# Two row scalings moved to VectorE, a token table and negated scores in a two-block kernel

## The chip, the cores and the metric

The kernel runs on one core of a Trainium2 chip. The metric is the device time of one execution in microseconds (us); the number given for a kernel is the median of its runs, and every run is one launch of the whole program.

## What is computed

The reference takes a sequence of 1024 tokens of width 1024 through two blocks. The part of the first block that matters here ends with a router and 32 experts:

```python
x = x + g1[:, None, :] * mix
h = modulate(x, sh2, sc2)          # rms_norm(x) * (1 + sc2) + sh2
x = x + g2[:, None, :] * hier_moe(h, ...)

g_prob = softmax(hf @ w_group + b_group)          # 4 groups, the best one is taken
e_logits = hf @ w_router + b_router               # 8 experts in a group, the best two are taken
...
out = segment_sum(ys * row_w[:, None], row_tok)   # two experts' rows come back to each token
```

The second block begins with sliding-window attention with a sink, 16 query heads on 4 key heads, blocks of 128 tokens:

```python
s = q @ k.T * HEAD_DIM ** -0.5 - slope * dist     # outside the window: -inf
m = maximum(max(s), sink)
p = exp(s - m)
denom = sum(p) + exp(sink - m)
o = (p / denom) @ v
```

After it come three further mixers and a feed-forward network, which the change does not touch.

## The kernel before

The program is one instruction stream per engine, planned ahead. A scheduler decides the order of most of it; some stretches are written inside a "manual schedule" context, where VectorE, ScalarE and GpSimd (the profile calls them DVE, ACT and POOL) run exactly in the order of the code. The tokens lie in 8 tiles of 128 rows. SyncE (SP) issues nearly all transfers, in the order of its own list, and indirect DMAs (gathers and scatters by a table of row numbers) are issued on POOL.

**Routing.** `phase2` finishes the output projection: `tile_half` (L807) makes half a tile with 24 matmuls (L812), scales it on DVE (L814) and adds it to `x1[t]` (L815). For each tile the router's logits follow: squares and their sums on ACT (`sq`, L966), the norm (`stat`, L971 and `rstd`, L225/L226), 8 transposes on PE (`tr`, L979) with two copies on ACT (L981), 8 matmuls of 36 columns (`mm`, L986) and one DVE operation (`lg`, L990). `h2_rows` (L1006) makes the modulated rows that the experts will gather, and SP writes them to DRAM (`h2d`, L1015) beside the tile itself (`x2d`, L1016). For tiles 0 to 5 that is two DVE operations on 128x1024 (L1010, L1014). For tiles 6 and 7 it is called with POOL as its engine, at the end of the manual stretch: ACT scales by the norm (L1012), POOL multiplies (L1013) and adds (L1014). The buffer is slot 26 or 27, by the parity of the tile.

`route` (L1021) is a generator of about 18 short DVE operations on two or four tiles' logits (L1037 to L1057), each of which needs the one before. The manual stretch hands them out with `some(n)` between the logits of tiles 6 and 7; then the last two tiles are routed, and `dispatch` (L1069) follows, one long dependent chain. It counts tokens per expert, writes the small integer list `ints` (L1134 to L1136) that SP reads to know which expert's weights to load, and builds the table of tokens: 16 one-hot squares of 128x128 (`soh`), the first six on POOL one by one (L1156), the others on DVE (L1152), and 16 matmuls (L1166) that sum `soh[q]` times `bv[q]` in one bank. The values in `bv` come from `val` (L912), twice the token number less 2048; three DVE operations (L1168, L1171, L1172) add 2048, turn the sum into integers and halve it, and that is `toki`. The first gathers on POOL (L1345) need `toki`, and so does SP: from a certain load on, the order of SP's list is tied to it (`self.hold`, L1172, used at L1316).

**Experts.** `phase4` streams the weights of the experts from DRAM (L1315), splits each into a high and a low part (ACT L1334, DVE L1335), multiplies, and adds the results to `x2d` with scatters on POOL (L1339). The scheduler orders this stage.

**Attention.** The loop at L1797 makes 32 steps (8 query blocks by 4 key heads) in manual order. Step `it` transposes the shares of step `it-3` (`turn`: PE L1773, ACT copy L1775, DVE masked copy L1778), makes the scores of step `it` (`scores`), the shares of step `it-1` (`share`), and the values of step `it-3` (PE L1789, ACT L1837, DVE L1838). `scores` is where the lines of the change lie: 4 custom DVE operations (L1744) add the bias to the scores and keep the row maximum in `am`; L1747 negates the four maxima into `anm`, and L1749 makes `aes`, the sink less the maximum:

```python
V.tensor_tensor_reduce(out=s_[:, i, 0:nk], in0=ps, in1=bias[kv][:, i, k0:256], scale=1.0,
                       scalar=sink[:, h:h + 1], op0=ALU.add, op1=ALU.max, accum_out=m[:, i:i + 1])
nm = self.W("anm", [P, 4])
V.tensor_scalar(nm, m, -1.0, None, op0=ALU.mult)
es = self.W("aes", [P, 4])
V.tensor_sub(es, sink[:, 4 * kv:4 * kv + 4], m)
```

`share` takes four exponentials on ACT with `anm` as their bias (L1757) and one of `aes` (L1759), sums and inverts on DVE (L1760, L1761), and lets POOL add the two halves of the window (L1763) and multiply by the inverse (L1764).

## Time and profile before

| | us |
|---|---|
| median of 3 runs | 2257.21 (2256.58 to 2259.82) |
| the profiled execution | 2255.42 |
| its span, first to last instruction | 2253.6 |
| mean granted TensorE clock in it | 0.962 of full speed |

| engine | busy us | share of the span | instructions |
|---|---|---|---|
| PE (matmul) | 2037.8 | 90% | 10594 |
| DVE | 1506.8 | 67% | 2292 |
| ACT | 905.8 | 40% | 1591 |
| POOL | 914.5 | 41% | 662 |

By time, the execution is: up to 427 us the first mixer, 427 to 538 the output projection, 538 to 590 routing and dispatch, 590 to 1190 the experts, 1190 to 1315 the projection for attention, 1315 to 1438 attention, and from there to 2253 the remaining mixers and the feed-forward network. The busy share is a mean over these stages, each with a limit of its own, so the stages are read one by one. In the chain of work that ended last, PE has 48%, DMA 18%, DVE 16% and "issue" (time in which an engine waited for nothing that the profile shows) 10%.

### The profile page before, as it was taken

Reading aid. Unit: us, or ns where it says so; the run is one execution under the profiler, and the core shown is the slowest. Engines: PE = TensorE matmul, PEld = TensorE weight load, DVE = VectorE, ACT = ScalarE, POOL = GpSimd, SP = SyncE. Lnnn points to the kernel's source line nnn. Section 1 sums busy time; section 2 is a strip of 40 time slices with the busy share of each in tenths; the row PEclk is TensorE's granted clock in tenths of the full one; section 3 lists DMA queues with packets and bytes.
Section 4 is the critical chain, followed back from the end, with each engine's and each line's share of the span. In section 5 each row is a group of like instructions: output and inputs, shape, how many; then the busy total and the mean of one; then the engine's idle time right before and its main releaser. Section 6 shows DMA issues by size and latency. Waiting matters only on the chain.

```text
span 2253.6 us, 30335 instructions
## 1 busy us (share of the span) xinstructions
PE 2037.8 (90%) x10594; PEld 1502.7 (67%) x10594; DVE 1506.8 (67%) x2292; ACT 905.8 (40%) x1591; POOL 914.5 (41%) x662
## 2 busy tenths in 40 slices
PE   4988999997899998998868997899999999989996
PEld 2677888886555654666526884587888787767774
DVE  7688886627454534667525449737787777599998
ACT  2544447412244333545315138634322232244433
POOL 2365252333211131212212027404666666567786
PEclk9999999998799999999989999999999999999998
DMA  7462111315899789999994310321454454575541
GB/s 264 126 187 79 30 37 47 114 55 219 311 389 347 280 302 392 381 342 376 381 341 132 131 29 10 122 94 57 131 185 165 145 186 142 166 269 176 193 153 75
DMA packets 204739, 426.09 MB, mean 189 GB/s; under 512 B 18580, under 2 KB 99202, under 8 KB 204578
## 3 DMA queue, kind: packets, MB, share of 16 engines
q1 hardware_dynamic: 195218, 402.62, 49.6%
q0 software_dynamic: 9360, 21.46, 4.1%
q8 instruction: 85, 1.39, 0.3%
q14 instruction: 76, 0.62, 0.1%
HBM read 361.36 MB, written 65.01 MB: 189 GB/s over the span
## 4 chain that ended last, share of the span: by engine, by line
PE 48%; DMA 18%; DVE 16%; issue 10%; POOL 5%; ACT 3%; SPq 0%; POOLq 0%; DVEq 0%; ACTq 0%
PE a L282 7%; DMA s<-w 6%; PE a L270 4%; PE a L812 4%; DMA x2d<-s,dstp 3%; DMA s<-w_ada 3%; PE t L1949 3%; PE a L1949 2%; PE a L1394 2%; PE r L1949 2%; DVE s L2152 2%; DVE s L1744 2%; PE a L1403 2%; PE t L1403 2%; DVE s L1934 1%
## 5 line engine op out<-in xcount | busy, mean ns | idle before, releaser
L1335 DVE TENSOR_TENSOR s<-s,s 128x1024 fp32r<-128x1024 f32 x168 | 207.2, 1243 | 123.8 <-ACT s L1334 120.4
L282 PE MATMUL a<-s,s 128*128 128x512 f32 x1008 | 243.4, 399 | 10.4 <-ACT s L503 10.4
L1334 ACT ACTIVATE s<-s 128x1024 fp32r<-128x1024 f32 x168 | 176.5, 1058 | 159.3 <-PE t L1394 60.5
L282 PEld LDWEIGHTS a<-s,s 128*128 128x128 f32 x1008 | 189.5, 190 | 52.6 <-ACT s L503 10.8
L1934 DVE TENSOR_TENSOR s<-s,s 128x512 fp32r<-128x512 f32 x154 | 162.5, 1072 | 73.3 <-ACT s L1933 73.3
L1949 PE MATMUL t<-s,s 128*128 128x512 f32 x648 | 162.4, 406 | 14.9 <-DVE s L1934 9.9
L1949 PE MATMUL a<-s,s 128*128 128x512 f32 x708 | 172.2, 393 | 0.3 <-DVE s L1934 0.2
L1345 POOL DMA_INDIRECT s<-h2d,toki x38 | 42.5, 1118 | 295.0 <-PE r L1376 142.4
L1949 PEld LDWEIGHTS t<-s,s 128*128 128x128 f32 x648 | 125.7, 195 | 46.8 <-DVE s L1934 11.4
L1933 ACT ACTIVATE s<-s 128x512 fp32r<-128x512 f32 x154 | 91.4, 623 | 159.4 <-DVE s L1934 71.7
L1949 PEld LDWEIGHTS a<-s,s 128*128 128x128 f32 x708 | 132.7, 188 | 31.4 <-DVE s L1934 0.6
L2152 DVE TENSOR_TENSOR s<-s,s 128x512 fp32r<-128x512 f32 x129 | 139.2, 1115 | 0.0
L1394 PE MATMUL t<-s,s 128*128 128x512 f32 x384 | 119.7, 402 | 3.7 <-DVE s L1478 1.8
L1949 PE MATMUL r<-s,s 128*128 128x512 f32 x492 | 120.2, 394 | 0.1
L1394 PE MATMUL a<-s,s 128*128 128x512 f32 x336 | 108.5, 416 | 8.2 <-DVE s L1478 5.0
L270 PE MATMUL a<-s,s 128*128 128x512 f32 x432 | 107.0, 399 | 2.6 <-DVE s L1593 2.6
L1949 PEld LDWEIGHTS r<-s,s 128*128 128x128 f32 x492 | 92.7, 189 | 21.9 <-DVE s L1934 0.5
L2151 ACT ACTIVATE s<-s 128x512 fp32r<-128x512 f32 x154 | 84.8, 622 | 41.5 <-POOL s L2152 18.2
L2317 PE MATMUL a<-s,s 128*128 128x512 f32 x348 | 94.9, 397 | 3.1 <-DVE s L2338 1.7
L2317 PE MATMUL t<-s,s 128*128 128x512 f32 x348 | 90.8, 399 | 7.5 <-DVE hraw L2329 2.0
L1403 PE MATMUL a<-s,s 128*32 128x256 f32 (+1 forms) x736 | 92.1, 468 | 4.9 <-ACT s L1377 3.0
L812 PE MATMUL a<-s,s 128*128 128x512 f32 x384 | 92.7, 397 | 0.6 <-DVE s L666 0.6
(579 smaller groups left out, 4407.7 us busy)
## 6 DMA issues: line engine op xcount, KB each, us to landing
s<-w SPq DMA_DIRECT2D x384, 512.0 KB
s<-w_ada SPq DMA_DIRECT2D x48, 512.0 KB
s<-ffn_w_gate_up SPq DMA_DIRECT2D x44, 512.0 KB
s<-fd SPq DMA_DIRECT2D x77, 256.0 KB
fd<-s SPq DMA_DIRECT2D x33, 512.0 KB
h2d<-s SPq DMA_DIRECT2D x24, 512.0 KB
s<-w_in SPq DMA_DIRECT2D x22, 512.0 KB
s<-ffn_w_down SPq DMA_DIRECT2D x22, 512.0 KB
```

The costliest lines, as they stand in the source:

```text
L270: nc.tensor.matmul(ps[:m], a[:, k, :], b(k, h), start=(k == 0 and n == 0), stop=(k == KC - 1 and n == 2))
L282: nc.tensor.matmul(ps[h][:m], a[:, k, :], b(k, h), start=(k == 0 and n == 0), stop=(k == KC - 1 and n == 2))
L812: nc.tensor.matmul(ps, a.of(k, t), W[k][:, b], start=(k == 0 and n == 0), stop=(k == 7 and n == 2))
L1334: nc.scalar.activation(hi, raw, AF.Copy)
L1335: V.tensor_sub(lo, raw, hi)
L1394: nc.tensor.matmul(pp[h], a[:, k // 4, s], w[:, h * 512:(h + 1) * 512], start=(k == 0 and n == 0), stop=(k == 7 and n == 2))
L1403: nc.tensor.matmul(p_[M * g:M * g + M, 0:N], x[:, k_, :], w[:, :, g, :], start=(k_ == 0), stop=(k_ == 7))
L1933: A.activation(t[:, 0], src, AF.Copy)
L1934: V.tensor_sub(t[:, 1], src, t[:, 0])
L1949: nc.tensor.matmul(ps, t[:, a, k], xs[k][:, b], start=(k == 0 and n == 0), stop=(k == 3 and n == 2))
L2152: (G if loads[1] % SHARE == SHARE - 1 else V).tensor_sub(u[:, 1], t, u[:, 0])
L2317: nc.tensor.matmul(ps[p], a[:, e, q * P:(q + 1) * P], b[:, f], start=(i == g[0] and n == 0), stop=(i == g[-1] and n == 2))
```

## The change

- The rows of tiles 6 and 7 for the experts are made on DVE alone. Tile 6 goes through `h2_rows` at the head of the manual stretch; tile 7 is multiplied by the modulation in two halves (`scaled`) and finished by one scalar_tensor_tensor once its norm is known. ACT's two scalings and POOL's four operations go. Fewer router steps stand between the logits of tiles 6 and 7, and `stat(7)` comes ahead of `lg(6)`.
- The token table holds tokens less 1024, not twice that, and one DVE operation turns the matmuls' sum into `toki` in place of three.
- POOL makes 3 of the 16 one-hot squares in place of 6, DVE the other 13; the matmuls take them in another order.
- Attention takes negated scores: the keys' factors, the bias, the mask and the sink change sign, the custom operation keeps the minimum, which is `anm` at once, so L1747 goes; `aes` is `anm` less the negated sink; the exponentials take a scale of -1.

```diff
@@ phase2 @@
+            def scaled(h):
+                sl = slice(512 * h, 512 * h + 512)
+                V.tensor_mul(h2[:, sl], self.x1[7][:, sl], self.sc2b[:, sl])
+
             sq(6, 0)
             sq(6, 1)
             stat(6)
             sq(7, 0)
+            self.h2_rows(6, V)
             tile_half(7, 1, W1, self.g1[1])
             steps = self.route(4, 6)
...
+            h2 = self.S(27)
+            scaled(0)
             some(2)
             tr(6, 0)
             tr(6, 1)
             mm(6, "t0")
             tr(7, 0)
-            some(4)
+            some(2)
             sq(7, 1)
             tr(7, 1)
-            some(3)
+            scaled(1)
+            some(2)
+            stat(7)
             lg(6)
-            stat(7)
+            some(2)
             mm(7, "a0")
+            V.scalar_tensor_tensor(h2, h2, self.rr[:, 7:8], self.sh2b, op0=ALU.mult, op1=ALU.add)
+            self.h2_out(7, h2)
             some(20)
             lg(7)
             for _ in self.route(6, 8):
                 pass
-            self.h2_rows(6, nc.gpsimd)
-            self.h2_rows(7, nc.gpsimd)
             self.dispatch()
@@ router constants, dispatch @@
-        nc.gpsimd.iota(vi, pattern=[[1, 2], [256, 8]], base=-2048, channel_multiplier=2)
+        nc.gpsimd.iota(vi, pattern=[[0, 2], [128, 8]], base=-1024, channel_multiplier=1)
-        for q in range(6):
+        for q in range(3):
             nc.gpsimd.tensor_scalar(soh[0][:, q], io128, plc[:, q:q + 1], None, op0=ALU.is_equal)
-        one(V, 6, 8)
+        one(V, 3, 8)
-        qs = [0, 1, 2, 3, 4, 5, 8, 9, 10, 11, 12, 13, 14, 15, 6, 7]
+        qs = [0, 8, 9, 10, 11, 1, 12, 13, 14, 15, 2, 3, 4, 5, 6, 7]
-        V.tensor_scalar(tf, pt[:, 0:NCOL], 2048.0, None, op0=ALU.add)
-        V.tensor_copy(self.toki, tf)
-        self.hold = V.tensor_scalar(self.toki, self.toki, 1, None, op0=ALU.logical_shift_right)
+        self.hold = V.tensor_scalar(self.toki, pt[:, 0:NCOL], float(T), None, op0=ALU.add)
@@ attention @@
+        V.tensor_scalar(sink, sink, -1.0, None, op0=ALU.mult)
...
             for i, h, ps in heads:
                 V.tensor_tensor_reduce(out=s_[:, i, 0:nk], in0=ps, in1=bias[kv][:, i, k0:256], scale=1.0,
-                                       scalar=sink[:, h:h + 1], op0=ALU.add, op1=ALU.max, accum_out=m[:, i:i + 1])
-            nm = self.W("anm", [P, 4])
-            V.tensor_scalar(nm, m, -1.0, None, op0=ALU.mult)
+                                       scalar=sink[:, h:h + 1], op0=ALU.add, op1=ALU.min, accum_out=nm[:, i:i + 1])
             es = self.W("aes", [P, 4])
-            V.tensor_sub(es, sink[:, 4 * kv:4 * kv + 4], m)
+            V.tensor_sub(es, nm, sink[:, 4 * kv:4 * kv + 4])
...
-                nc.scalar.activation(s_[:, i, 0:nk], s_[:, i, 0:nk], AF.Exp, bias=nm[:, i:i + 1],
+                nc.scalar.activation(s_[:, i, 0:nk], s_[:, i, 0:nk], AF.Exp, scale=-1.0, bias=nm[:, i:i + 1],
                                      accum_out=den[:, i:i + 1])
```

The lines of the changed file lie 9 to 11 further down there (L1010 is L1020, L1037 is L1048, L1744 is L1755), so names and shapes tell the rows below apart better than lines do. In these rows `s_` with a number is a slot of SBUF, `a_`, `t_` and `r_` are PSUM banks, and the words in brackets are the queues or engines whose count the instruction waits for.

On DVE, where the manual stretch begins, the rows of tile 5 (`s_3997` from `x1[5]`, `s_3270`) are followed before by the last operations of tile 7's projection and by the router:

```order
L1010 SCALAR_TENSOR_TENSOR s_3997<-s_3270,rr,s_3521 128x1024 [waits DMAHW7_49,DMAHW4_49,Pool_49]
L1014 TENSOR_TENSOR s_3997<-s_3997,s_3534 128x1024 [waits DVE_49]
L1057 TENSOR_TENSOR s_3561<-s_3489 128x128 [waits PE_49]
L814 TENSOR_TENSOR hraw<-a_4013,m 128x512 [waits PE_49]
L815 TENSOR_TENSOR s_3274<-s_3274,hraw 128x512 [waits DMASW2_49,DMASW3_49,DMASW1_49,DMAHW4_49,DMASW0_49,DVE_49]
L990 SCALAR_TENSOR_TENSOR s_3488<-t_3987,rr,br 128x36 [waits PE_49]
L1037 TENSOR_REDUCE s_3488<-s_3488 128x2 [waits DVE_49]
L1039 TENSOR_TENSOR s_3489<-s_3488 128x8 [waits DVE_49]
```

and in the changed kernel by this:

```order
L1020 SCALAR_TENSOR_TENSOR s_3997<-s_3270,rr,s_3521 128x1024 [waits DMAHW7_49,DMAHW4_49,Pool_49]
L1020 SCALAR_TENSOR_TENSOR s_4013<-s_3272,rr,s_3521 128x1024 [waits DMAHW1_49,Pool_49]
L1021 TENSOR_TENSOR s_3997<-s_3997,s_3534 128x1024 [waits DVE_49]
L1021 TENSOR_TENSOR s_4013<-s_4013,s_3534 128x1024 [waits DVE_49]
L1068 TENSOR_TENSOR s_3561<-s_3489 128x128 [waits PE_49]
L814 TENSOR_TENSOR hraw<-a_4018,m 128x512 [waits PE_49]
L815 TENSOR_TENSOR s_3274<-s_3274,hraw 128x512 [waits DMASW2_49,DMASW3_49,DMASW1_49,DMAHW4_49,DMASW0_49,DVE_49]
L1001 SCALAR_TENSOR_TENSOR s_3488<-t_3987,rr,br 128x36 [waits PE_49]
L851 TENSOR_TENSOR s_4046<-s_3274,s_3521 128x512 [waits DMAHW6_49]
L1048 TENSOR_REDUCE s_3488<-s_3488 128x2 [waits DVE_49]
```

The two operations on tile 6 (`s_4013`) now stand among those on tile 5, and the first half of tile 7 (`s_4046`, L851) stands ahead of the router's first step, with a wait on the DMA queue DMAHW6. The slot of `s_4046` is that of `s_3997`: slot 27.

On SP the transfers of this stretch stand so before (`s_4276` is the zero tile, `s_4141` and `s_4147` the rows of tiles 6 and 7):

```order
L1315 DMA s_4297<-w 128x1024 [waits DMAHW3_49,PE_49]
L1315 DMA s_4299<-w 128x1024 [waits DMAHW4_49,PE_49]
L1015 DMA h2d<-s_3997 128x1024 [waits DMAHW5_49,DVE_49]
L1291 DMA x2d<-s_4276 128x1024 [waits DMAHW6_49,Pool_49]
L1315 DMA s_4301<-w 128x1024 [waits DMAHW7_49,PE_49,Activation_49]
L1315 DMA s_4303<-w 128x1024 [waits DMAHW0_49,PE_49,Activation_49]
L1016 DMA x2d<-s_3274 128x1024 [waits DMAHW1_49,DVE_49]
L1015 DMA h2d<-s_4141 128x1024 [waits DMAHW2_49,Pool_49]
L1015 DMA h2d<-s_4147 128x1024 [waits DMAHW3_49,Pool_49]
L1503 TENSOR_LOAD ints [waits DVE_49]
```

and so in the changed kernel:

```order
L1324 DMA s_4291<-w 128x1024 [waits DMAHW3_49,PE_49]
L1324 DMA s_4293<-w 128x1024 [waits DMAHW4_49,PE_49]
L1300 DMA x2d<-s_4270 128x1024 [waits DMAHW5_49,Pool_49]
L1026 DMA h2d<-s_3997 128x1024 [waits DMAHW6_49,DVE_49]
L1324 DMA s_4295<-w 128x1024 [waits DMAHW7_49,PE_49,Activation_49]
L1324 DMA s_4297<-w 128x1024 [waits DMAHW0_49,PE_49,Activation_49]
L1026 DMA h2d<-s_4013 128x1024 [waits DMAHW1_49,DVE_49]
L1027 DMA x2d<-s_3274 128x1024 [waits DMAHW2_49,DVE_49]
L1026 DMA h2d<-s_4046 128x1024 [waits DMAHW3_49,DVE_49]
L1512 TENSOR_LOAD ints [waits DVE_49]
```

The zero tile goes ahead of the rows of tile 5, which take its place on queue DMAHW6, and the rows of tiles 6 and 7 wait for DVE in place of POOL. Further on, the scheduler places some 540 of PE's 8420 rows in the expert stage differently, with the matching rows on DVE, ACT and POOL; SP's own list of loads there is unchanged.

In the attention loop, one step on DVE reads so before (the ISA rows are the custom operation and the read of its accumulator; the last of the four pairs is shown):

```order
L1744 ISA s_14691,am<-a_14693,s_14170,sink 128x256
L1744 ISA am 128x1
L1747 TENSOR_SCALAR anm<-am 128x4 [waits DVE_49]
L1749 TENSOR_TENSOR aes<-sink,am 128x4
L1760 TENSOR_TENSOR aden<-aden,aes 128x4 [waits Activation_49,Pool_49]
L1761 RECIPROCAL aden<-aden 128x4 [waits DVE_49]
```

and so in the changed kernel:

```order
L1755 ISA s_14791,anm<-r_14793,s_14167,sink 128x256
L1755 ISA anm 128x1
L1758 TENSOR_TENSOR aes<-anm,sink 128x4 [waits DVE_49]
L1769 TENSOR_TENSOR aden<-aden,aes 128x4 [waits Activation_49,Pool_49]
L1770 RECIPROCAL aden<-aden 128x4 [waits DVE_49]
```

The negation is gone, and nothing has taken its place; each of ACT's exponentials now waits for a custom operation of its own.

## Rows read from the trace of the kernel before

**Rows 1.** Stretches: us; busy us of PE, PEld, DVE, ACT, POOL; clock, DMA share, GB/s.
```profile
590.00:700.00 110.00, 107.38 (x502) 55.86 (x500) 49.58 (x52) 44.63 (x56) 18.69 (x14) 0.99 1.00 379
...
1351.00:1438.00 87.00, 68.86 (x489) 37.44 (x488) 85.35 (x343) 74.36 (x272) 59.67 (x54) 1.00 0.08 27
```

**Rows 2.** Timeline of DVE, 533 to 578: start, duration, instruction, idle before it.
```profile
533.69 1.28 DVE L1010 SCALAR_TENSOR_TENSOR s<-s,rr,s 128x1024 f32<-128x1024 f32 x1 [0.18 <-POOL rr L226]
535.01 1.23 DVE L1014 TENSOR_TENSOR s<-s,s 128x1024 f32<-128x1024 f32 x1
...
539.27 0.69 DVE L815 TENSOR_TENSOR s<-s,hraw 128x512 f32<-128x512 f32 x1
...
544.53 0.26 DVE L990 SCALAR_TENSOR_TENSOR s<-t,rr,br 128x36 f32<-128x36 f32 x1 [1.53 <-PE t L986]
...
545.19 0.22 DVE L1045 TENSOR_TENSOR s<-s 128x64 f32<-128x64 f32 x1
...
546.73 2.33 DVE L1045 TENSOR_TENSOR s<-s 128x64 f32<-128x64 f32 x1
549.09 2.38 DVE L1057 TENSOR_TENSOR s<-s 128x64 bf16<-128x64 f32 x1
551.40 0.24 DVE L990 SCALAR_TENSOR_TENSOR s<-a,rr,br 128x36 f32<-128x36 f32 x1
...
551.87 1.84 DVE L1039 TENSOR_TENSOR s<-s 128x8 f32<-128x8 f32 x1
...
554.14 2.00 DVE L1045 TENSOR_TENSOR s<-s,s 128x8 f32<-128x8 f32 x1
```

**Rows 3.** Timeline of POOL, same stretch.
```profile
546.62 2.35 POOL L1013 TENSOR_TENSOR s<-s,s 128x1024 f32<-128x1024 f32 x1 [0.71 <-ACT s L1012]
...
568.09 5.73 POOL L1156 TENSOR_SCALAR s<-s,s 128x128 fp32r<-128x128 f32 x6 [11.97 <-DVE s L1147]
```

**Rows 4.** Timeline of SP's issues, 533 to 592.
```profile
536.26 0.33 SPq L1015 DMA_DIRECT2D h2d<-s  x1
...
566.00 15.32 SPq L1315 DMA_DIRECT2D s<-w  x13
```

**Rows 5.** DMA view, 536 to 552.
```profile
DMA packets 968, 3.51 MB, mean 219 GB/s; under 512 B 112, under 2 KB 112, under 8 KB 967
```

**Rows 6.** Timeline of DVE and of PE in dispatch.
```profile
570.57 1.71 DVE L1152 TENSOR_TENSOR s<-s,s 128x512 fp32r<-128x512 f32 x3
576.46 0.22 DVE L1168 TENSOR_SCALAR s<-a 128x58 f32<-128x58 f32 x1 [4.19 <-PE a L1166]
...
573.87 2.55 PE L1166 MATMUL a<-s,s 128*128 128x58 f32 x11 [0.16 <-POOL s L1156]
```

**Rows 7.** Waits of SP's queue, 565 to 592: us in total, times, longest.
```profile
SPq L1315 <- DVE toki L1172: 1.0, 1, 1.0
```

**Rows 8.** Busy time by stretch, within the experts (columns as in rows 1).
```profile
780.00:800.00 20.00, 16.99 (x76) 8.96 (x76) 7.72 (x9) 5.69 (x8) 5.26 (x4) 0.91 0.15 35
```

**Rows 9.** Timeline of DVE in the attention loop, 1420 to 1434.
```profile
1424.94 0.15 DVE L1749 TENSOR_TENSOR aes<-sink,am 128x4 f32<-128x4 f32 x1
...
1425.60 0.68 DVE L1778 TENSOR_TENSOR hraw<-t,tri 128x512 f32<-128x512 f32 x1
...
1427.93 0.66 DVE L1747 TENSOR_SCALAR anm<-am 128x4 f32<-128x4 f32 x1
```

**Rows 10.** Timeline of ACT and of POOL in the same stretch.
```profile
1425.14 0.51 ACT L1757 ACTIVATE s<-s,anm 128x256 f32<-128x256 f32 x1 [0.35 <-DVE aes L1749]
...
1427.67 0.60 ACT L1775 ACTIVATE m<-t 128x512 f32<-128x512 f32 x1
1428.71 0.51 ACT L1757 ACTIVATE s<-s,anm 128x256 f32<-128x256 f32 x1 [0.44 <-DVE aes L1749]
...
1427.30 1.27 POOL L1763 TENSOR_TENSOR s<-s 128x512 f32<-128x512 f32 x1 [0.73 <-ACT s L1757]
```

**Rows 11.** Groups by line and shape on DVE, 1351 to 1438: busy us, mean ns.
```profile
L1747 DVE TENSOR_SCALAR anm<-am 128x4 f32<-128x4 f32 x24 | 15.5, 647 | 0.8
```

19 lines of the change are left out of this document (9 added, 10 removed).

## The prediction

> **What bounds the kernel now.** I read the busy time by stretch first, then the engines' timelines in the two stretches that the change touches. The experts, 590 to 1190 us, are bound by the weights' stream: in 590 to 700 the DMA share is 1.00 and PE is busy 107.38 of 110 us, while the other engines are busy less than half of it [rows 1]. Both are full, so either way an earlier start counts, and the smaller shift of the two is what passes. The stream starts when `ints` is known: SP issues its 13 loads from 566.0 on [rows 4], and on the way waits 1.0 us for `toki` [rows 7]. So what routing gains should pass through the experts to the end, as far as it moves SP. In attention, 1351 to 1438, DVE is busy 85.35 of 87 us [rows 1], but part of that is holding: the negation of four columns takes 0.647 us on average, 24 times [rows 11], though the subtraction on the same four columns takes 0.15 [rows 9].
>
> Both places show the same thing. In routing, L1045 on 128x64 takes 0.22 us alone and 2.33 at 546.73; it ends at 549.06, just behind POOL's L1013, which ends at 548.97 [rows 2, 3]. In attention the negation issued at 1427.93 ends at 1428.59, just behind POOL's L1763, which ends at 1428.57 [rows 9, 10]. Four router steps are held so [rows 2]; reductions and scalar_tensor_tensors between them are not.
>
> **Routing, to the last logits.** From L815's end (539.96) to the logits of tile 7 (551.40) pass 11.44 us [rows 2]. In them are 2.11 and 2.16 us of holding (2.33 and 2.38 less 0.22) and a wait of 1.53 for tile 6's logits; 5.64 are DVE's own. POOL's four operations go, so the holds go. The 1.53 go too: PE now transposes tile 6 earlier, and DVE is later.
>
> Added on DVE: ahead of L815, two more 128x1024 operations, 1.28 and 1.23 [rows 2]. Between L1014's end (536.24) and L815's start (539.27) lie 3.03 us with about 1.0 of work, so 2.0 are waiting that covers them, and 0.5 show. Behind L815, two halves at 0.69 each, like L815, the closing operation at 1.28 like L1010, and some 0.3 for the norm of tile 7, which POOL finishes: 3.0.
>
> The new wait: the first half goes into slot 27, and must wait until the rows of tile 5 have been read from there by their transfer. It stands in DVE's in-order list, and behind it queue all router steps of tiles 4 to 7. That transfer is issued about 537.6 (533.69 and three operations, 1.28, 1.28 and 1.23 [rows 2]; 1.3 later than the 536.26 of rows 4), and the zero tile is now ahead of it. Landing alone at the 379 GB/s of the full stream [rows 1], its 0.5 MB take 1.4 us: it would be there at 539 and cost nothing, since DVE arrives at 541. If all 3.51 MB that move between 536 and 552 [rows 5] must pass first, at 379 GB/s that is 9.3 us: 545.3, a wait of 4.3. It shares the engines with the zero tile and with two weight loads issued right behind it, so it is nearer the late end: 544, a wait of 3.0. Sum: +0.5 - 2.11 - 2.16 - 1.53 + 3.0 + 3.0 = +0.7.
>
> **Routing, behind the last logits.** Two more holds go: 1.84 and 2.00, less at most 0.22 each [rows 2]: -3.4. So `ints` is known 2.7 us earlier (between 1.4 and 5.7 by the two ends of the wait). ACT's two scalings go at no gain: ACT is idle there. POOL's list has nothing behind them before the squares.
>
> **Dispatch.** POOL needs 5.73 us for six squares, 0.96 each, from 568.09 to 573.82; DVE makes ten in 1.71 us, 0.17 each, and is done at 572.28 [rows 3, 6]. The last 11 matmuls wait for POOL and take 2.55, 0.23 each [rows 6]. With three squares POOL is done at about 571; DVE has three more, 0.5 us, and ends at 572.8; five matmuls follow, to 574.1 in place of 576.4: -2.3. Two DVE operations of about 0.22 behind the matmuls go [rows 6]: -0.45. `toki` comes 2.7 + 2.75 = 5.5 us earlier. SP gains less: its own list of value reads and loads starts 2.7 earlier, and only the 1.0 that it waited for `toki` [rows 7] can go as well: **-3.7**. The first expert's matmuls need `toki` and shift by its 5.5, the stream by SP's; I take SP's, the smaller. If the stream slides as it is, its holes slide with it.
>
> The Trainium skill, GPSIMD Engine Reference, "Key points", calls VectorE about twice as fast as GpSimd for elementwise work. By that, POOL's six squares would take 2.1 us, DVE's would always end last, and the dispatch term would be +0.5 in place of -2.3, the whole sum 1.1 less of a gain; the trace disagrees, 0.96 against 0.17.
>
> **Experts.** The scheduler has placed some 540 PE rows anew. Work and bytes are the same, so I cost it at nothing, with ±5 us: the holes in the stream are of that size. The largest, 780 to 800 with a DMA share of 0.15, is 17 us [rows 8].
>
> **Attention.** A step takes 3.57 us (the exponentials start at 1425.14 and 1428.71 [rows 10]). The loop is: exponentials, 2.16 until POOL's addition starts (1427.30), 1.27 for it, then 0.14 until the held negation has released the next exponentials. The change takes the negation out, and the exponentials wait for the custom operations alone. The next limit: ACT's own list, from the exponentials to the end of the copy `m` (1428.27), is 3.13 [rows 10], which would give 0.44 × 24 = 10.6 us. But `aes` is now the first operation behind the customs, it reads two operands of SBUF as L1045 does, and I expect it to be held by the same POOL addition, until 3.43 after the exponentials' start. Behind it on DVE stand `aden`, the inverse, L1838 and `hraw`: from L1749 to `hraw`'s end 1.34 us (1424.94 to 1426.28 [rows 9]), 1.27 without L1749's own start; from `hraw`'s end over PE's values and the next transposes to the copy `m` 1.39 (1427.67 [rows 10]); the copy 0.60; then exponentials again. That loop spans two steps: 3.43 + 1.27 + 1.39 + 0.60 = 6.69, some 0.05 less as ACT overlaps, 3.32 a step. Gain 0.25 × 24 = **-6.0**, bounds 0 (a hold that moves and still decides) and -10.6. The other edits there cost nothing: signs folded into existing operations, and one operation on the sink of 16 columns early in the program, beside PE's work.
>
> The Trainium skill, SBUF — State Buffer, "Who interferes with whom", says a VectorE instruction with two SBUF inputs contends with a GpSimd instruction that reads SBUF, for the whole instruction. By that, `aes` is held as taken above, and the step is 3.32 rather than 3.13; the trace agrees for L1045, 2.33 against 0.22.
>
> **Sum.** -3.7 - 6.0 = -9.7. The profiled execution took 2255.42, so about 2245.7 in a profile; the median shown is 1.8 above it, so the forecast is **2247.5**.
>
> **Rivals.**
> - *More of both.* The transfer from slot 27 has landed when DVE arrives (-3.0 more on `ints` and SP), and `aes` slips through between POOL's operations, as the copy of ACT becomes the bound (-4.6 more): 2240. For it: 0.5 MB alone would be early. Against: the loads beside it, and L1045's rows.
> - *The new wait eats routing.* The rows of tile 5 land behind everything issued beside them, at 545.3 or later, up to 548; `ints` then gains 1.4 or nothing, SP at most 2.4. With attention as above: 2250. For it: the queue is in order, and the zero tile moves ahead.
> - *The hold only changes its victim.* `aes` in the negation's place leaves the loop at 3.57; routing alone gives 2253.5. For it: the same POOL addition; against: the exponentials no longer need what is held.
> - *Slower.* The new order of the experts opens another hole in the weights' stream. Its place: a stretch where SP's next load waits for PE to free a buffer, as in 780 to 800; its price: 17 us by that row, 2264.5. It decides from 14.2 us of added idle DMA on (9.7 given back, and 4.5 more). For it: 540 rows moved. Against: the same loads in the same order, and a stream that is full elsewhere.
> - *It does not do what it says.* The schedule shows the operations where the change puts them, and nothing is left of the negation; only its waits are open, and these are the cases above.
>
> **How the numbers follow.** A measurement of this kernel tells 0.2% from no change, 4.5 us: 2252.7 to 2261.7. The forecast has 0.60, with its own range 2242 to 2252.5 (±5 for the experts); more of both 0.13, all faster; routing eaten 0.12, three quarters of it faster; the hold moved 0.09, a third faster; slower 0.06. Faster: 0.60 × 0.97 + 0.13 + 0.09 + 0.03 = 0.83; slower 0.05, since a smaller hole would only cancel the gain; same 0.12. The range is 2239 to 2255: it leaves out part of the strongest case, the slow one, and the top of the moved hold.
>
> **What would show it.** In the changed profile: the router's steps at 0.16 to 0.26 us each, none at 2; DVE idle ahead of the first L851, released by a DMA, 3 us; TENSOR_LOAD of `ints` followed by SP's loads from about 563.3, `toki` at about 571.6; the experts' end some 4 us earlier at an unchanged DMA share. In attention no negation, `aes` stretched to some 0.3 us or more and ending with POOL's L1772, steps of 3.3 us. Wrong would be: steps still at 3.57; a DVE wait beyond 6 us; an expert stage that ends no earlier, or later, although its loads start earlier.

## The result, and the profile after

The changed kernel takes **2236.19 us** (median of 4 runs, 2234.0 to 2236.91) against 2256.89 for the kernel before beside it: ratio 0.9895, interval 0.9877 to 0.9914, 20.7 us less. That is 11 us more than forecast, and lies below the range. The profiled execution took 2236.43 us (span 2234.6, clock 0.963) against 2255.42: 18.99 us less. By stretches of these two executions, in us (from the start of the program to the start of the last L814; to the last cast of `ints`; to the last transfer that reads `x2d`, which I call the expert stage; to the first `aden` of attention; to its last; to the end):

| kernel | to L814 | to ints | experts | projection | attention | rest |
|---|---|---|---|---|---|---|
| before | 538.54 | 26.43 | 624.25 | 132.53 | 120.71 | 811.17 |
| changed | 542.10 | 21.90 | 612.75 | 131.80 | 113.51 | 812.58 |
| difference | +3.56 | -4.53 | **-11.50** | -0.73 | -7.20 | +1.41 |

The first and the last column aren't touched by the change and vary so from one execution to the next. Routing gained 4.5 (forecast 2.7), attention 7.2 (6.0), and the experts, which I had costed at nothing, 11.5.

*Routing.* The timeline of DVE in the changed kernel, 537 to 556, answers to [rows 2]:

```profile
537.23 2.48 DVE L1020 SCALAR_TENSOR_TENSOR s<-s,rr,s 128x1024 f32<-128x1024 f32 x2 [0.18 <-POOL rr L226]
539.63 2.35 DVE L1021 TENSOR_TENSOR s<-s,s 128x1024 f32<-128x1024 f32 x2
...
542.82 0.69 DVE L815 TENSOR_TENSOR s<-s,hraw 128x512 f32<-128x512 f32 x1
...
546.79 0.69 DVE L851 TENSOR_TENSOR s<-s,s 128x512 f32<-128x512 f32 x1 [2.75 <-DMA h2d<-s]
...
553.53 0.22 DVE L1056 TENSOR_TENSOR s<-s 128x64 f32<-128x64 f32 x1
553.79 0.23 DVE L1068 TENSOR_TENSOR s<-s 128x64 bf16<-128x64 f32 x1
553.93 0.25 DVE L1001 SCALAR_TENSOR_TENSOR s<-a,rr,br 128x36 f32<-128x36 f32 x1
...
555.01 0.17 DVE L1056 TENSOR_TENSOR s<-s,s 128x8 f32<-128x8 f32 x1
```

No router step is held: the operation that took 2.33 takes 0.22, and the one that took 2.00 takes 0.17. The new wait is there, 2.75 us for the transfer out of slot 27. The two more operations on 128x1024 cost nothing: from the first L1020 to L815 pass 5.59 us, before 5.58 [rows 2].

*Dispatch and SP.* Timelines of POOL, DVE and PE in the changed kernel, 565 to 575 [rows 3, 6], then SP's issues [rows 4]:

```profile
567.12 3.54 POOL L1167 TENSOR_SCALAR s<-s,s 128x128 fp32r<-128x128 f32 x3 [16.62 <-DVE s L1158]
...
569.60 2.11 DVE L1163 TENSOR_TENSOR s<-s,s 128x512 fp32r<-128x512 f32 x3
573.77 0.22 DVE L1181 TENSOR_SCALAR toki<-a 128x58 int32<-128x58 f32 x1 [2.07 <-PE a L1177]
...
569.82 3.91 PE L1177 MATMUL a<-s,s 128*128 128x58 f32 x16 [4.45 <-DVE s L1170]
```
```profile
565.03 30.13 SPq L1324 DMA_DIRECT2D s<-w  x18
```

Of the squares DVE's now end last (571.71, POOL's 570.66), and PE's sixteen matmuls, back to back from 569.82 to 573.73, end 2.0 us behind them. SP issues 18 loads in a row; the wait for `toki` of [rows 7] is gone. Before's six squares on POOL [rows 3] were of two kinds: the first four took 4.55 us, and the last two, with DVE's squares done at 572.28, 1.18 together:

```profile
572.64 1.18 POOL L1156 TENSOR_SCALAR s<-s,s 128x128 fp32r<-128x128 f32 x2
```

*Attention.* The timeline of DVE in the changed kernel, 1405 to 1419, with POOL's additions behind it, and the group of `aes` over the whole loop [rows 9 to 11]:

```profile
1405.69 0.17 DVE L1758 TENSOR_TENSOR aes<-anm,sink 128x4 f32<-128x4 f32 x1
...
1408.71 0.75 DVE L1758 TENSOR_TENSOR aes<-anm,sink 128x4 f32<-128x4 f32 x1
...
1412.30 0.16 DVE L1758 TENSOR_TENSOR aes<-anm,sink 128x4 f32<-128x4 f32 x1
...
1415.31 0.66 DVE L1758 TENSOR_TENSOR aes<-anm,sink 128x4 f32<-128x4 f32 x1
...
1418.81 0.17 DVE L1758 TENSOR_TENSOR aes<-anm,sink 128x4 f32<-128x4 f32 x1
...
1408.16 1.27 POOL L1772 TENSOR_TENSOR s<-s 128x512 f32<-128x512 f32 x1 [0.83 <-ACT s L1766]
...
1414.68 1.27 POOL L1772 TENSOR_TENSOR s<-s 128x512 f32<-128x512 f32 x1
```
```profile
L1758 DVE TENSOR_TENSOR aes<-anm,sink 128x4 f32<-128x4 f32 x30 | 13.5, 452 | 1.0
```

`aes` is held in every second step, until POOL's addition ends (1409.46 and 1409.43, 1415.97 and 1415.95), and steps of 3.0 and 3.5 to 3.6 us alternate: 13.12 us for four, 3.28 each, before 3.57.

*Experts.* Busy time by stretch, of before and of the changed kernel: the first row of each goes from `ints` to load 129 of the weights' stream (of the 372 behind `ints`), the second is 10 us that begin with a matmul about 140 us behind `ints`, the third goes from load 129 to the end of the stage (columns as in [rows 1]).

```profile
565.00:797.60 232.60, 213.01 (x1040) 126.09 (x1042) 115.60 (x153) 89.47 (x115) 44.66 (x36) 0.91 0.87 323
705.55:715.55 10.00, 9.31 (x28) 6.92 (x29) 3.63 (x5) 3.10 (x4) 1.00 (x1) 0.50 0.65 251
797.60:1189.20 391.60, 338.51 (x2241) 202.97 (x2237) 202.95 (x234) 154.43 (x203) 85.66 (x57) 0.93 0.99 363
```
```profile
564.00:786.10 222.10, 206.00 (x1033) 121.76 (x1035) 115.58 (x151) 89.00 (x115) 41.61 (x33) 0.93 0.90 337
703.71:713.71 10.00, 9.16 (x40) 6.47 (x40) 6.85 (x8) 4.70 (x7) 1.01 (x1) 0.83 0.58 232
786.10:1176.80 390.70, 337.76 (x2248) 202.39 (x2245) 201.71 (x235) 154.11 (x203) 85.45 (x58) 0.93 1.00 365
```

Of the 11.5 us, 10.5 are there by load 129; PE does nearly the same number of matmuls in it (1040, 1033) and is busy 7.0 us less and idle 3.5 us less. The rest of the stage differs by 0.9. The second kind of row shows a place where the clock is at its lower level, 0.50, in one kernel and 0.83 on average in the other. What follows is the search for the cause.

### The profile page after: what moved, and what is told of

It is laid out like the page before. It is cut to its first block, busy times and chain, and to the rows that moved or that the text cites. A ratio compares the mean times of both kernels' runs of the same rounds, so it can differ in the third digit from the quotient of the medians.

```text
span 2234.6 us, 30292 instructions
## 1 busy us (share of the span) xinstructions
PE 2031.7 (91%) x10594; PEld 1499.3 (67%) x10594; DVE 1496.2 (67%) x2264; ACT 901.4 (40%) x1589; POOL 902.2 (40%) x655
## 4 chain that ended last, share of the span: by engine, by line
PE 41%; DMA 21%; DVE 18%; issue 10%; POOL 5%; ACT 3%; SPq 1%; POOLq 0%; DVEq 0%; ACTq 0%
DMA s<-w 9%; PE a L282 7%; PE a L270 4%; PE a L812 4%; DMA x2d<-s,dstp 3%; DVE s L1943 2%; PE t L2326 2%; PE a L2326 2%; DMA s<-w_ada 2%; DMA s<-ffn_w_gate_up 2%; DMA x2d<-s,dsti 2%; PE a L1412 2%; DVE s L2161 2%; DVE s L509 1%; PE r L2326 1%
## 5 line engine op out<-in xcount | busy, mean ns | idle before, releaser
L1403 PE MATMUL t<-s,s 128*128 128x512 f32 x384 | 119.5, 407 | 5.3 <-DVE s L1487 3.1
L1403 PE MATMUL a<-s,s 128*128 128x512 f32 x336 | 106.5, 413 | 7.0 <-DVE s L1372 3.5
```

Of the source, the lines that this page charges most:

```text
L1403: nc.tensor.matmul(pp[h], a[:, k // 4, s], w[:, h * 512:(h + 1) * 512], start=(k == 0 and n == 0), stop=(k == 7 and n == 2))
```

## Experiments: the parts apart

**e1_attention, e8_attention_again**: the kernel before with the attention part of the change alone.

```diff
...
-                                       scalar=sink[:, h:h + 1], op0=ALU.add, op1=ALU.max, accum_out=m[:, i:i + 1])
-            nm = self.W("anm", [P, 4])
-            V.tensor_scalar(nm, m, -1.0, None, op0=ALU.mult)
+                                       scalar=sink[:, h:h + 1], op0=ALU.add, op1=ALU.min, accum_out=nm[:, i:i + 1])
...
```

> Only the attention part of the change (negated scores), routing and experts as before; the expert stage's instruction order is that of before. Theory of the moved hold: steps of 3.26 us in place of 3.57, 24 of them, so 6 to 7.5 us faster than before (about 2250). Rival, the gain of the whole change sits in attention and what follows: 15 us faster or more. Rival, the hold only moves: within 1 us of before.

> The attention part alone once more, with more rounds, since in e1 the attention stretch was 7.2 us shorter while the median was only 1.0 below before and its interval reached from 6.5 faster to 0.7 slower. Theory, executions differ by several us in the first 435 us, which no edit here touches: 5 to 8 us faster. Rival, the negation of the sink or the scheduler's list costs the first stretch what attention gains: 0 to 2 us faster, and a first stretch longer than 438 us again.

Measured: 0.9987 (0.9971 to 1.0003) and, in more runs, 0.9975 (0.9962 to 0.9989; 2252.8 against 2258.19). The attention stretch took 113.51 and 113.53 us in the two profiles, as in the changed kernel, the experts 624.16 and 624.49. So the stretch gains 7.2, although the medians show 1.0 and 5.4: in both profiles the stretch to L814, where nothing is changed, took 545.71 and 548.40 us instead of 538.54.

**e11_before_again, e12_changed_again, e10_third_order** asked whether that is the attention edit's doing. The last is the changed kernel with four memsets (`hraw`, 128x512, DVE) in front of `scaled(0)`, idle work that also flips the scheduler's order of the experts.

```diff
+            for _ in range(4):
+                V.memset(self.W("hraw", [P, 512]), 0.0)
             scaled(0)
```

> The kernel before, once more, for its first 540 us. Theory, the first stage differs from execution to execution by the length for which TensorE runs at half clock around 410 to 435 us: the end of the output projection anywhere in 538 to 549, and all stages behind it within 1 us of the first profile. Rival, the 545.7 and 548.4 of the two attention runs are due to that edit: 538 to 542 here.

> The changed kernel once more, beside e9 and e10 on the same chip. From the end of the output projection on, every stage within 1 us of its first profile (634.65, 131.8, 113.5, 812.6), and 18 to 23 us faster than before in the median.

> The changed kernel with four memsets of 128x512 on DVE ahead of the first half of tile 7, where DVE stands idle for 2.75 us anyway; they cost nothing or under 1 us. The scheduler then writes nearly the third order, 49 rows from e9's. Theory of the order: the expert stage after ints takes what it takes in e9, within 3 us, whatever the start; the total says whether this order beats the changed kernel's (below 2233) or not (above 2239).

Measured: 2253.49 in a single execution, 2235.58 (0.9894, 0.9878 to 0.9911) and 2248.07 (0.9954, 0.9938 to 0.9971). To L814 pass 538.99, 543.49 and 546.28 us: executions with the attention edit span 539.79 to 548.40, those without it 538.54 to 541.88, so it is no constant price of the edit. On the mean it is 543.2 against 540.5 us; whether a part of that belongs to the edit stays open. The stages behind it did not repeat within 1 us, as I had expected: the experts took 622.05 in e11 and 609.73 in e12, 2.2 and 3.0 us less than in the first profiles, and e12's projection took 134.68 in place of 131.80. A difference of 3 us in one profile of the expert stage is therefore no more than noise. The last run missed its number too: its experts took 615.79 us and e9's, in nearly the same order, 624.78 (below).

**e2_table_squares, e9_table_alone**: the table and POOL's three squares, and the table by itself.

```diff
-        nc.gpsimd.iota(vi, pattern=[[1, 2], [256, 8]], base=-2048, channel_multiplier=2)
+        nc.gpsimd.iota(vi, pattern=[[0, 2], [128, 8]], base=-1024, channel_multiplier=1)
...
-        for q in range(6):
+        for q in range(3):
...
```

> Only dispatch is changed: the table of tokens and 3 squares on POOL; the rows of tiles 6 and 7 stay on ACT and POOL, and the expert stage keeps the order of before. Theory of the order (most of the unforeseen gain is the expert stage's new order): toki 2.7 us earlier, SP at most 1.0, total 1 to 3 us faster. Rival theory of the start (the experts gain from toki and the first gathers coming earlier, whatever the order): more than 4 us faster, since toki takes about 40% of its whole shift here.

> The kernel before with the table of tokens alone: two DVE operations of 0.2 us less behind the matmuls of dispatch, nothing else. toki comes 0.45 us earlier, ints and SP's first loads not at all. But the scheduler writes a third order of the expert stage, 252 of PE's rows away from that of before and 238 from the changed kernel's, and in it no gate or down matmul stands between the eight transposes and the 16 matmuls that free the buffer SP waits for longest. Theory of the hole (the 9 matmuls that stand there before, and what they wait for, make the hole in the weights' stream): SP's longest wait 23 to 27 us in place of 32.5, load 129 of the stream 7 to 11 us earlier after ints, and up to 10 us faster in all, less what the third order does later. Rival theory of the start: within 1 us of before.

Measured: 0.9987 (0.9969 to 1.0005) and 0.9991 (0.9975 to 1.0006). `toki` stands 9.76 us behind the cast of `ints` with both, 11.49 with the table alone, 11.97 before; the experts take 621.03 and 624.78. Neither shows in the time.

**e3_rows**: the rows of tiles 6 and 7 on DVE alone, the rest as before.

```diff
...
+            self.h2_rows(6, V)
...
-            self.h2_rows(6, nc.gpsimd)
-            self.h2_rows(7, nc.gpsimd)
...
```

> Only the rows of tiles 6 and 7 on DVE; dispatch with six squares on POOL and three operations, attention as before. The expert stage's order is nearly that of the changed kernel. Theory of the order: ints 4 us earlier, and the new order on top, 11 to 15 us faster. Rival theory of the start: toki moves 4 of its 6.7 us, so 6 to 9 us faster. If the new wait on slot 27 were what matters: 3 us or less.

Measured: 2241.57, 0.9934 (0.9915 to 0.9953). `ints` 5.4 us earlier, experts 613.50 us, PE's order there that of the changed kernel but for 21 rows. This part alone carries 15 of the 20.7 us, and the expert stage's share comes with it.

## Experiments: an earlier start, or another order

Two things come with that part: the experts start earlier, and the scheduler orders them otherwise. Small idle operations on DVE flip the order with nothing else changed, and another slot or work on POOL moves the start. "Order" says whose order PE has in this stage, and how many of its rows differ from that.

**e4_slot35** gives tile 7's rows a slot of their own, so that the wait of 2.75 us goes; **e5_slot35_order_after** and **e6_slot35_order_before** add two and four memsets on DVE ahead of the dispatch.

```diff
-            h2 = self.S(27)
+            h2 = self.S(35)
...
+            for _ in range(2):
+                V.memset(self.W("hraw", [P, 512]), 0.0)
             self.dispatch()
```

> The changed kernel with the rows of tile 7 in slot 35 in place of 27, so that DVE's first half need not wait for the rows of tile 5 to be read. The wait of 2.75 us goes; ints and toki come 2.7 us earlier. The expert stage's order moves by 94 of PE's rows against the changed kernel. Theory that an earlier start passes through the experts: 2 to 3 us faster than the changed kernel (about 2233.5), plus or minus what the order does. Rival, the order decides: off from that by more than 4 us in either direction.

> Slot 35 for the rows of tile 7, as in e4, and two memsets of 128x512 on DVE ahead of dispatch; with them the scheduler writes the expert stage in exactly the changed kernel's order. Theory of the order: from the end of the output projection to the last read of x2d the changed kernel took 634.65 us; here 2.75 for the wait go and about 0.7 for the memsets come, so 632 to 633, and the total 1 to 3 us below the changed kernel's. Rival, e4's loss of 6.5 us in that stretch came from the slot or from the early start and not from the order: 639 to 642 again.

> The same with four memsets in place of two; now the scheduler writes the expert stage in the order of before, all but 3 of PE's rows, while ints and toki come as early as in the changed kernel or a little earlier. Theory of the order: only the start's share of 4 to 6 us is gained in the stretch, 644 to 647 us of it (before 650.68), and the total is 11 to 14 us faster than before. Rival theory of the start: 634 us or less, 20 us faster in all.

**e7_pool_holds** puts four additions of 128x1024 on POOL under the router of the changed kernel, which holds DVE again and delays `ints`, in the changed kernel's order.

```diff
             some(20)
+            for _ in range(4):
+                nc.gpsimd.tensor_add(self.S(36), self.x1[6], self.x1[7])
```

> The changed kernel with four additions of two 128x1024 tiles on POOL into a free slot, as many and as long as before's, so that DVE's router steps are held again; the expert stage's order is exactly the changed kernel's. Theory of the order: the stretch grows by the holds alone, 4 to 8 us on 634.65, so 639 to 643. Rival theory of the start (a threshold between the start of before and that of the changed kernel): back to 650.

| run | order | L814 to ints | experts | time, us | ratio |
|---|---|---|---|---|---|
| e4 | its own, 94 rows from the changed | 20.43 | 620.76 | 2242.11 | 0.9938 (0.9914 to 0.9962) |
| e5 | as changed | 21.07 | 616.30 | 2233.70 | 0.9904 (0.9879 to 0.9929) |
| e6 | as before, but for 3 rows | 22.15 | 625.05 | 2244.83 | 0.9943 (0.9927 to 0.9960) |
| e7 | as changed | 30.57 | 613.26 | 2244.71 | 0.9949 (0.9932 to 0.9965) |
| e10 | its own, 49 rows from e9's | 22.22 | 615.79 | 2248.07 | 0.9954 (0.9938 to 0.9971) |
| e12, changed again | as changed | 22.00 | 609.73 | 2235.58 | 0.9894 (0.9878 to 0.9911) |
| e11, before again | as before | 26.39 | 622.05 | 2253.49 | a single execution |

The order decides, and the start does not: e6 starts as early as the changed kernel and needs 625 us, e7 starts 4 us later than before and needs 613. The start passes nearly one to one beside it (e7: `ints` 8.7 us later, the time 8.5, and the way from L814 to the stage's end 9.2 in the profiles). e4 missed its number, with an order of its own: it has load 129 at 223.7 us behind `ints`, as early as the changed kernel but for 1.6, and loses its 8 us behind that, at places that I did not look for. In e5 the stage took 616 and not the 611 that I expected. All times of this stage in the old order lie between 621 and 625, in the changed one between 610 and 616.

e7 also shows the hold itself, brought back. Timeline of POOL, then of DVE, 548 to 560:

```profile
549.21 10.46 POOL L885 TENSOR_TENSOR s<-s,s 128x1024 f32<-128x1024 f32 x4
```
```profile
552.79 2.12 DVE L1058 TENSOR_TENSOR s<-s 128x64 f32<-128x64 f32 x1
554.94 2.38 DVE L1068 SCALAR_TENSOR_TENSOR s<-s 128x64 f32<-128x64 f32 x1
557.36 0.22 DVE L1050 TENSOR_REDUCE s<-s 128x2 f32<-128x64 f32 x1
557.62 2.13 DVE L1052 TENSOR_TENSOR s<-s,s 128x64 f32<-128x64 f32 x1
```

## Experiments: what the order costs

SP's longest wait in this stage is the one for load 129, for PE to free a buffer: 32.5 us in before, 26.0 in the changed kernel. Before has a matmul group (L1446) of nine ahead of the matmuls that free it; the order of e9 has none there, yet e9 takes 624.78 (load 129 came 4 us earlier in place of 7 to 11, and the rest of the stage lost that again): that first explanation fell. PE's own timeline shows two pauses. Here is the first, in before: DVE from 702 on, then PE.

```profile
702.41 2.36 DVE L1335 TENSOR_TENSOR s<-s,s 128x1024 fp32r<-128x1024 f32 x2
704.80 0.69 DVE L1415 TENSOR_TENSOR hraw<-hraw,t 128x512 f32<-128x512 f32 x1
...
705.55 1.11 PE L1425 MATMUL r<-ident,hraw 128*128 128x128 f32 x4 [3.66 <-DVE hraw L1415]
707.35 1.22 PE L1446 MATMUL a<-s,s 128*128 128x512 f32 x2 [0.69 <-ACT s L1430]
```

and in the changed kernel:

```profile
701.71 1.23 DVE L1344 TENSOR_TENSOR s<-s,s 128x1024 fp32r<-128x1024 f32 x1
702.96 0.69 DVE L1424 TENSOR_TENSOR hraw<-hraw,t 128x512 f32<-128x512 f32 x1
...
703.71 0.66 PE L1434 MATMUL r<-ident,hraw 128*128 128x128 f32 x4 [2.52 <-DVE hraw L1424]
705.05 1.28 PE L1455 MATMUL a<-s,s 128*128 128x512 f32 x3 [0.69 <-ACT s L1439]
```

PE waits 3.66 us, because DVE's list has two weight splits ahead of the product that PE needs; in the changed kernel it has one, and PE waits 2.52. Behind it the clock falls to its lower level, 0.50, and stays there longer in before: two 128x512 matmuls take 1.22 us there, and 0.73 where the clock is full (e14, below). The second pause, 228 us behind `ints`, is in before and not in the changed kernel; here one split stands ahead of the eviction (L1464) that PE needs:

```profile
790.61 1.23 DVE L1335 TENSOR_TENSOR s<-s,s 128x1024 fp32r<-128x1024 f32 x1 [0.25 <-ACT s L1334]
791.75 0.74 DVE L1464 SCALAR_TENSOR_TENSOR s<-t,gt,x 128x512 f32<-128x512 f32 x1
...
792.64 3.02 PE L1446 MATMUL t<-s,s 128*128 128x512 f32 x9 [3.01 <-DVE s L1464]
```

Over all profiles the first pause goes with the stage's time: in the seven where it is 3.65 or 3.66 us (before, e1, e2, e6, e8, e9, e11) the experts take 621 to 625, in all others 610 to 621; e9 and e10, 49 rows apart, have 3.65 and 2.52. That is no test yet. The runs that follow start from before's order and take work out of DVE's list in front of these two points. **e13_one_split** and **e14_no_split** have one and two splits behind the product (the scheduler is told to issue them after it); **e15_second_pause** has one more split behind the eviction L1464; **e16_second_pause_gone** two there, and ACT's half of one. The diff is that of e16 (`mul` is the product, `yv` and `ya` the evictions on DVE and ACT, `spi` counts the splits); e13 has 33 alone in place of (33, 34), e15 has 59 alone in place of (58, 59), and e13 to e15 go without its first two lines; the last condition is in e15 and e16 only.

```diff
+                if self.spi in (59,):
+                    es.enter_context(self.tc.issue_after(self.ya.ins))
                 nc.scalar.activation(hi, raw, AF.Copy)
+                if self.spi in (33, 34):
+                    es.enter_context(self.tc.issue_after(self.mul.ins))
+                if self.spi in (58, 59):
+                    es.enter_context(self.tc.issue_after(self.yv.ins))
                 V.tensor_sub(lo, raw, hi)
...
```

> The kernel before with one of the experts' weight splits on VectorE (the pair of L1335, L1336 of one slice) issued behind a gated product instead of ahead of it: of the two splits that stand ahead of the eviction hraw about 140 us after ints one is taken away, and TensorE's order of matmuls stays as before but for two rows. Theory (TensorE's pause at that point, and the lower clock behind it, carry the order's cost): the pause falls from 3.66 us to about 2.5 as in the changed kernel, the granted clock over the next 10 us rises from 0.50 towards 0.83, load 129 of the stream comes about 228 to 229 us after ints instead of 232.6, and the kernel is 3.5 to 5 us faster than before; the remaining 5 to 7 us of the order's cost stay. Rival (only the order as a whole counts, this pause is made up later): load 129 within 1.5 us of 232.6 and the time within 2 us of before.

> As the run with one split taken away, with the second one behind a product as well, so that no split stands ahead of that eviction. Theory: TensorE's pause there falls to about 1.3 us, the clock over the next 10 us is 0.83 or more, load 129 comes 227 to 229 us after ints, and the kernel is 4 to 6 us faster than before. Rival (the pause is made up later): within 2 us of before.

> The run without a split ahead of the eviction, with one more split moved: about 227 us after ints, the split that stands ahead of the eviction L1464 on VectorE goes behind it; TensorE's order is unchanged. Theory (the pauses and the clock behind them carry the order's cost): TensorE's pause there falls from 3.01 to about 1.8 us, load 129 comes at 223 to 225 us after ints (226.1 without this, 222.1 in the changed kernel), and the kernel is 1 to 3 us faster than the run without a split, 6 to 9 us faster than before. Rival (only the first pause matters): load 129 at 226 and 4 to 6 us faster than before.

> As the run with the second pause shortened, with two splits on VectorE and one on ScalarE behind that eviction: nothing but the small split of the gated product stands ahead of it. TensorE's order differs from the old one in 11 rows. Theory: the pause falls from 3.01 to 0.5 to 1 us, load 129 comes at 221 to 224 us after ints as in the changed kernel, the stage from ints to the last read of x2d takes 612 to 616 us as there (616.9 and 617.6 in the two runs without splits at the first pause, 624.25 before), and the kernel is 8 to 11 us faster than before. Rival (the rest of the order's cost lies elsewhere): 616 to 618 us for the stage and 4 to 6 us faster than before.

**e17_all_old_order** is the changed kernel in slot 35 with four memsets, as e6, and e16's edits.

> All parts of the changed kernel, but with the experts in the old order (the rows of tile 7 in slot 35 and four small memsets on VectorE in front of the dispatch bring it back, as in an earlier run that took 2244.8 us) and with the two pauses of TensorE shortened by the same moved splits as in the last run. Theory (the two pauses are what the old order costs): the stage from ints to the last read of x2d takes 612 to 616 us instead of the 625.05 of that earlier run, and the kernel takes 2233 to 2237 us, 0.988 to 0.991 of before, as the changed kernel does. Rival (the changed kernel's order is worth something beyond the pauses): a stage of 618 or more and a time over 2240.

| run | first pause, second | load 129 behind ints | experts | time, us | ratio |
|---|---|---|---|---|---|
| before | 3.66, 3.01 | 232.6 | 624.25 | | |
| e13 | 2.52, 3.0 | 226.9 | 616.88 | 2253.20 | 0.9991 (0.9977 to 1.0005) |
| e14 | 1.26, 3.01 | 226.1 | 617.58 | 2250.30 | 0.9975 (0.9959 to 0.9991) |
| e15 | 1.3, 1.52 | 223.0 | 618.29 | 2251.64 | 0.9963 (0.9949 to 0.9976) |
| e16 | 1.3, 1.52 | 223.4 | 614.66 | 2248.56 | 0.9952 (0.9933 to 0.9970) |
| e17 | 1.3, 1.5 | 222.6 | 611.39 | 2234.44 | 0.9896 (0.9879 to 0.9914) |
| changed | 2.52, none | 222.1 | 612.75 | 2236.19 | 0.9895 (0.9877 to 0.9914) |

PE's first pause in e14 and its second in e15, and the stretches: of e13 the 10 us behind the first pause and the way from `ints` to load 129, then that way alone in e14, in e15 and in e11, which is before again.

```profile
705.09 0.66 PE L1427 MATMUL r<-ident,hraw 128*128 128x128 f32 x4 [1.26 <-DVE hraw L1417]
706.43 0.73 PE L1448 MATMUL a<-s,s 128*128 128x512 f32 x2 [0.69 <-ACT s L1432]
```
```profile
787.07 2.33 PE L1450 MATMUL t<-s,s 128*128 128x512 f32 x9 [1.52 <-ACT s L1471]
```
```profile
706.50:716.50 10.00, 9.31 (x84) 5.17 (x84) 2.70 (x4) 1.80 (x4) 1.00 (x1) 0.66 0.99 358
567.00:794.00 227.00, 209.20 (x1040) 124.92 (x1042) 115.71 (x154) 89.34 (x115) 45.76 (x36) 0.92 0.89 331
566.90:793.00 226.10, 209.73 (x1040) 124.73 (x1042) 115.55 (x153) 89.31 (x115) 46.05 (x36) 0.92 0.89 332
567.40:790.40 223.00, 208.03 (x1040) 123.97 (x1042) 115.55 (x154) 89.32 (x115) 44.20 (x35) 0.92 0.90 335
565.40:797.00 231.60, 212.01 (x1040) 125.75 (x1042) 115.52 (x153) 89.38 (x115) 44.24 (x36) 0.92 0.87 323
```

*The first pause.* One split moved takes 5.7 us off the time to load 129, for the same 1040 matmuls: PE is busy 3.8 us less (213.01 to 209.20) and idle 1.8 us less, and the clock in the 10 us behind the pause is 0.66 in place of 0.50. But the edit changed more than the pause. The expectation has PE's order as before but for two rows, and the traces show otherwise. Of 24 matmuls of L1446, before has 18 within 11 us behind the pause; e13 has 2 there, and the other 22 start 14.6 us behind it, after 64 small ones. PE in before, then in e13 (L1448 is L1446 there, L1405 is L1403):

```profile
710.34 5.87 PE L1446 MATMUL a<-s,s 128*128 128x512 f32 x14
...
716.58 3.66 PE L1403 MATMUL t<-s,s 128*32 128x256 f32 x64
```
```profile
711.02 5.18 PE L1405 MATMUL t<-s,s 128*32 128x256 f32 x64
...
721.15 4.45 PE L1448 MATMUL a<-s,s 128*128 128x512 f32 x18
```

Counted in the programs as built, some 75 of PE's matmuls stand elsewhere in e13 than in before, some 95 in e17, and some 330 in the changed kernel. So e13 does not show what the pause and the clock are worth by themselves. A part of its gain is neither: e11 has the same mean clock up to load 129 as e13, 0.92, and still load 129 comes 4.6 us later there, where the longer pause is 1.1 and PE is busy 2.8 us more. e14 has e13's order on PE exactly; there the second split alone makes the pause 1.26 us shorter, with the clock at 0.66 in both, and it brings 0.8.

*The second pause.* e15 has e14's order on PE exactly, so this step is clean: 1.49 us less of pause bring load 129 3.1 us earlier, 1.7 of it in PE's busy time for the same matmuls and 1.4 in its idle time. The clock in the 10 us behind the pause is 1.00 in e15 and e16, and 0.83 in before, e13, e14 and e17. In e15's profile the stage lost these 3 us again by load 204, in e16's it kept them. e16's further edit left the pause at 1.52, not at the 0.5 to 1 that I expected, since ACT and no longer DVE releases PE there, in e15 already.

*The whole.* By the medians the four runs are 2.3, 5.2, 7.5 and 10.6 us faster than before, the first within its uncertainty, below the 3.5 I expected; the profiles of the stage show 7.4, 6.7, 6.0 and 9.6, all clear of the 621 to 625 of the old order, but one profile each does not rank them. And e17, with everything else of the changed kernel, the old order but for what the moved splits reorder, and both pauses shortened, comes out where the changed kernel does. So the splits that stand ahead of these two evictions carry the difference between the orders; the changed order has no other value that these runs show. How the share of the first place divides between the pause, the clock behind it and the matmuls that moved with the split is not shown. e5 and e17 lie 2 us below the changed kernel, less than can be told apart.

## Why the prediction was wrong

- **The experts.** The step that failed is "I cost it at nothing, with ±5 us", and the reason given for it, the same work and bytes. The new order was worth 11.5 us in the profiles. In its place the runs showed that a new order changes what PE waits for: splits on DVE ahead of two evictions, and with these moved, an order that is otherwise the old one takes what the new one takes (e16, e17). The rows that would have warned of it were in the trace of before: PE's pauses of 3.66 and 3.01 us, each behind DVE's list, and the clock at 0.50 behind the first; I looked for holes in the weights' stream and not for what stands ahead of an eviction that PE waits for. The rival "another hole in the stream" had the right place and the wrong sign. Had ±12 stood there, the range would just have held the time.
- **Routing to the last logits**, forecast +0.7: from L815's end to them 10.42 us in place of 11.44, so -1.0. The 0.5 for the two more operations fell to nothing, since the wait they fill was long enough, and the wait for slot 27 was 2.75, not 3.0; the rest is the 3.0 added on DVE, part of which must have lain in gaps; that part I have not traced. The holds went as stated, and e7 brings them back with POOL's work.
- **Behind the last logits**, forecast -3.4: 13.57 to 10.07, -3.5. Right.
- **Dispatch**, forecast -2.75: from the cast of `ints` to `toki` 11.97 to 9.77, -2.2. The step that failed is the five matmuls, 1.3 us, behind the last square: PE's sixteen run back to back from 569.82 and end 2.0 us behind DVE's last square, so PE's own list ends last, and neither POOL's speed (1.18 for a square in place of 0.96) nor DVE's (0.16) counts there. The Trainium skill, GPSIMD Engine Reference, "Key points", has VectorE about twice as fast for elementwise work. The trace again disagrees: 1.18 against 0.16, seven times, and between three and four times where DVE is done. For in before the last two of POOL's six squares, behind DVE's last, took 0.59 each, and the four ahead of them, beside DVE's operations, 1.14 each. In the changed kernel all three run beside these. That looks like the hold in the other direction; no run tests it.
- **SP**, forecast -3.7: its loads start 4.5 us earlier within the routing, as `ints` does, and that passes to the end, as stated (e7, in the other direction).
- **Attention**, forecast -6.0: -7.2 in every profile that has it. The mechanism was right: `aes` is held in one step of two, the loop spans two steps, and a step takes 3.28 where 3.32 was worked out. The Trainium skill, SBUF — State Buffer, "Who interferes with whom", calls the ports that VectorE and GpSimd share an exclusive lock; the trace agrees, `aes` ends within 0.03 us of POOL's addition. The rival in which the hold only changes its victim fell.
- **The new wait eats routing** fell: DVE was released at 546.79, which is 543.2 in before's time (the changed profile is 3.56 later at L814), ahead of the 545.3 from which that rival starts; the forecast's 544 was close.

With the measured terms the sum is -4.5 - 11.5 - 7.2 = -23.2, -0.7 in the projection, and +5.0 in the stretches that vary between executions: the 18.99 of the profiles.

## What to carry to other kernels

Where a scheduler orders a stage anew, "the same work and bytes" bounds nothing: list PE's longest waits in that stage, look at what stands ahead of the releasing instruction on its engine, and at the granted clock behind each, and take their sum as the uncertainty. A weight split of 1.2 us ahead of an eviction cost 0.8 to 5.7 us by load 129 here, the most where it reordered PE's list as well. Compare the order that was built before calling a run "the same order". To tell an order from an earlier start, flip the one with idle operations and move the other with a delay.

## What the runs showed of the hardware

What a pause of PE costs is not its length. In two steps that leave PE's order as it is, 1.26 us less of pause gave 0.8 by load 129 with the clock behind it at 0.66 in both (e13 to e14), and 1.49 us less gave 3.1 with the clock at 1.00 in place of 0.83 (e14 to e15). The length of the pause alone does not fix how long the clock stays low. Over 10 us behind it the mean clock is

- 0.50 behind 3.66 us (before), and 0.66 behind 3.65 in the same order (e1);
- 0.83 behind 2.52 (changed kernel), and 0.66 behind 2.52 in the same kernel again (e12);
- 0.66 behind 1.26 (e14), and 0.83 behind 1.26 (e17);
- 0.83 behind the second pause of 3.01 in before, and 1.00 behind it in e11.

What decides it stays open. The time at the lower level also makes the untouched start of the program vary. In two executions, 410 to 435 us, busy throughout or nearly so, the mean clock is 0.90 (before) and 0.53 (e8), and the second reaches L814 9.9 us later:

```profile
410.00:435.00 25.00, 23.36 (x138) 20.27 (x139) 17.27 (x29) 11.49 (x19) 7.28 (x6) 0.90 0.22 75
```
```profile
410.00:435.00 25.00, 25.00 (x114) 22.83 (x115) 12.77 (x22) 9.39 (x16) 8.05 (x7) 0.53 0.19 62
```

So a few us of one profile can come from there, and stretches are to be compared one by one. A scalar_tensor_tensor is held by POOL too (2.38 us in e7); the prediction had it among the operations that are not, from rows of before.
